# Low parts of the second mixer's a, g and k weights kept in DRAM, and its convolution taps traced at 1.2 steps per tile

## The chip, the cores and the metric

The kernel runs on one core of one Trainium2 chip. Its time is the device time of one execution in microseconds (us). The profile is of one more execution of the same program.

## What is computed

`reference` runs two blocks. The first one has two layers; each is a mixer and a feed-forward, with a post-normalisation behind each. In layer 0 the two streams (256 rows of `x` and 256 rows of context) go through everything; in layer 1 the context only gives the mixer its keys, values and states, and `x` alone goes on. The mixer projects the rows with one wide `w_in`, and merges three branches: attention, gated linear attention and a convolution of width 31 over 1024 channels. Cut to the parts of the layer 1 mixer that matter:

```python
def _latent_mixer(h, mem, cos, sin, p):
    proj = h @ p['w_in']          # k, v, kg, vg, glr | q, qg, r, glu (a and g), gates
    ...
    return _merge(o_att, o_gla, r, glu, gates, p), ...

def _conv_module(glu, p):
    a, g = jnp.split(glu, 2, axis=-1)
    y = a * jax.nn.sigmoid(g)
    y = lax.conv_general_dilated(y, p['conv_w_dw'], ...) + p['conv_b_dw']   # 31 taps, each channel alone
    y = jax.nn.silu(_layernorm(y, p['conv_ln_g'], p['conv_ln_b']))
    return y @ p['w_conv_o']
```

The second block has two smaller layers; the change doesn't touch them. All is in fp32.

## The kernel before

A product in fp32 is made of three matmuls of fp32r operands: with each operand split in a high part (a cast) and a low part (the rest), the high weights meet the high and the low rows, and the low weights meet the high rows. `mm_fm` (weights stationary, channels on the output's partitions) issues them in lines 386 to 388, `mm_tm` (rows stationary) in lines 467 to 469. Weights come as raw fp32 (`load_raw`, line 354, 1 MB for 256 columns, two buffers), and `wsplit` makes `whi` by a ScalarE cast (line 362) and `wlo` by a VectorE subtract (line 288), 128x1024 at a time and with three buffers each. `fm` does so for `mm_fm`, `proj_tm` for `mm_tm`. Every DMA is issued on SP's queue.

Nearly all else (activations, tables, intermediate rows) lies in a pool `u` of 71 slots of 2 KB per partition. A scheduler orders the instructions of all engines ahead of time in a simulated time, by priorities that follow the order in which the program traces them; `self.pri(d)` shifts the priority, and a negative d is earlier. Slow work beside the matmuls is traced by "lanes": `bg(name, generators, rate)` starts one, and each tile of a projection calls `tick`, which traces `rate` steps of every lane; `flush` traces what is left.

The mixer of layer 1 (`mixer(1, ...)`) goes as follows. Eight tiles of a and eight of g (each a product of 128 columns by 256 rows: 8 blocks x 3 matmuls), alternating two and two. After the first pair, `conv_taps` loads the convolution's weights (`cwr`, line 1307), TensorE transposes them (line 1311) and VectorE writes `cw`. After each pair of channels m, m+1 the lane "conv" gets a generator `conv`: its taps `ca<-gt,cw,ca` (line 291, at priority +600) come in 15 steps of 4, so 60 steps in all at `CRATE1` = 1.0 steps for each tile. Then k and v (4 tiles), q (8), the small gate rows (1), kg (4), qg (4), vg (8), and merge(0) (16 tiles: 8 gates and 8 of `w_att_o`), which give 12 ticks of the a/g stage after its first four tiles and 45 more. After merge(0), `flush("gla", "conv")` traces the taps that are left; the last step of the last pairs sums the channels into `cs` on GpSimd. Then `conv_norm` runs in the lane: TensorE sums the columns of `cs` (line 1347), and squares, scale and low parts follow, while merge(2) computes its gates and then needs the result for `w_conv_o`. The scores of the gated linear attention (`eq`, `ek`: GpSimd, VectorE, ScalarE) are traced in the same stretch.

The feed-forward of layer 0 (about 840 to 1160 us) has two halves of `ffn_up` (12 and 10 pairs of tiles of 128 columns by 512 rows) with a down projection between them: 24 + 12 + 20 = 56 ticks. The lane "ada" (loads `aw`, 256 KB each) runs there. `flush("ada")` stands behind it.

Of the kernel before, what the change touches and what calls it, by code (L numbers as in the profile page):

```python
# [9 lines left out]
F32 = mybir.dt.float32  # L10
# [15 lines left out]
CRATE1 = 1.0  # L26
# [4 lines left out]
CP = 600  # L31
PLO0A = 0
# [155 lines left out]
class Builder:  # L188
    NU = 71

    def __init__(self, ctx, tc, ins, out, dbg=None, stop=None):
        self.tc, self.nc, self.I, self.out = tc, tc.nc, ins, out
        self.dbg, self.stop = dbg, stop
        self.n = 0
        self.lanes = {}
        self.pool_lo = 0
        self.nsplit = 0
        self.wpri = WP
        self.behind = None
        self.fheld = None  # L200
        self.spare = {}
        self.lo_behind = []
        self.hook = self.lo_after = None
        self.ns = [None]
        P = lambda **k: ctx.enter_context(tc.tile_pool(**k))
        self.cp = P(name="cp", bufs=1)
        self.sp = P(name="sp", bufs=12)
        self.up = P(name="up", bufs=self.NU)
        self.wp = P(name="wp", bufs=2)
        self.rp = P(name="rp", bufs=2)  # L210
        self.hp = P(name="hp", bufs=3)
        self.lp = P(name="lp", bufs=3)
        self.pm = P(name="pm", bufs=3, space=PSUM)
        self.ps = P(name="ps", bufs=5, space=PSUM)
# [142 lines left out]
    def wsplit(self, src, shape, pri=None):  # L357
        hi = self.hp.tile(list(shape), F32R, tag="whi", name=self.nm("whi"))
        lo = self.lp.tile(list(shape), F32R, tag="wlo", name=self.nm("wlo"))
# [9 lines left out]
    def fm(self, w, c0, ncols, nk=8):  # L369

        raw = None
        for m in range(ncols // 128):
# [3 lines left out]
            yield self.wsplit(raw[:, :, o : o + 128], (128, nk, 128))  # L376

    def mm_fm(self, out, W, a, nk=8, first=True, last=True):
# [5 lines left out]
        for k in range(nk):  # L384
            mm = self.nc.tensor.matmul
            mm(out, lhsT=hi[:, k, :], rhs=a.hi[k], start=(first and k == 0), stop=False)  # L386
            mm(out, lhsT=hi[:, k, :], rhs=a.lo[k], start=False, stop=False)  # L387
            mm(out, lhsT=lo[:, k, :], rhs=a.hi[k], start=False, stop=(last and k == nk - 1))  # L388
# [82 lines left out]
    def proj_tm(self, specs, nk, a, tts, consumer, hold=0, mid=None, between=None, ks=None, late=None, held=None, need=None, hook=False):  # L471
# [8 lines left out]
        for part, kl in enumerate((ks[: nk - hold], ks[nk - hold :])):  # L480
# [8 lines left out]
            for h, (w, r0, c0, ncols) in enumerate(specs):  # L489
                for run in runs:  # L490
# [6 lines left out]
                    for k2 in range(0, n4, 2):  # L497
# [3 lines left out]
                        hi, lo = self.wsplit(raw[:, k2 : k2 + n2, :], (128, n2, ncols))  # L501
                        for t in tts:
                            for k in range(n2):
                                kk = run[k2 + k]
                                self.mm_tm(ps[t, h], a, t, kk, (hi[:, k, :], lo[:, k, :]), kk == ks[0], kk == ks[-1])
# [1254 lines left out]
    def layer1(self, l):  # L1760
# [33 lines left out]
        if l == 0:  # L1794
            self.bg("ada", [self.ada(1, (1, 0, 4, 3, 2, 5))], AD1)
        if T == 512:
# [10 lines left out]
            self.flush("ada")  # L1807
# [373 lines left out]
```

## Time and profile before

| | us |
|---|---|
| median of 3 executions | 2539.07 |
| lowest and highest of them | 2538.33 and 2540.02 |
| the profiled execution | 2540.03 |
| its span, first to last instruction | 2538.2 |

| engine | busy us of the span | share |
|---|---|---|
| TensorE, matmul | 2405.4 | 95% |
| TensorE, weight load | 2066.3 | 81% |
| VectorE | 1624.2 | 64% |
| ScalarE | 1180.4 | 47% |
| GpSimd | 521.2 | 21% |

Shares of the whole span are means over stages with different limits. The feed-forward of layer 0 lies at 840 to 1160 us, a and g of the second mixer at 1217 to 1282, k, v and q at 1282 to 1345, attention and vg at 1345 to 1470, merge(0) at about 1470 to 1520, and merge(2) begins there. "Granted clock" is the share of full speed at which TensorE was allowed to run. In the rows PE is TensorE, PEld its weight loads, DVE VectorE, ACT ScalarE, POOL GpSimd, SP or SPq the queue that issues DMAs.

### The profile page before, as it was taken

To read this page: it belongs to the slowest core of one execution; us is meant where nothing else is said; L and a number is where in the kernel's file an instruction comes from. 1 tells how busy PE (TensorE), PEld (TensorE's weight loads), DVE (VectorE), ACT (ScalarE), POOL (GpSimd) and SP (SyncE) were. 2 spreads that over 40 slices of the span, in tenths; PEclk is the share of its full clock that TensorE was granted. 3 is DMA by queue.
4 is the path that set the end of the run, shared out by engine and by line. 5 is a ranking of instruction groups with operands and counts; after the bars stand their busy time and mean duration, and the time that the engine had idled before them with its cause. 6 is when DMAs were issued, how large, how long until landed. Compare 5 with 4: busy or idle time off the path is not lost. (4 is left out here: it accounts for less than half of the span.)

```text
span 2538.2 us, 38571 instructions
## 1 busy us (share of the span) xinstructions
PE 2405.4 (95%) x15163; PEld 2066.3 (81%) x15163; DVE 1624.2 (64%) x2700; ACT 1180.4 (47%) x2225; POOL 521.2 (21%) x460
## 2 busy tenths in 40 slices
PE   7989999899999999999889987998999999999998
PEld 4767887688877777778879887888987899887997
DVE  5878997984365433343899597676625656556564
ACT  3223577654343322232536945654443644446443
POOL 1002003790014000003310006531072100102001
PEclk9999999999999999999999998999999999999999
DMA  8432212223433545553342252643664246543454
GB/s 256 150 136 73 84 31 90 67 84 117 133 102 131 183 150 183 166 183 100 92 129 92 68 166 84 196 137 96 211 208 149 85 150 219 198 144 106 153 192 149
DMA packets 277689, 345.39 MB, mean 136 GB/s; under 512 B 12894, under 2 KB 208888, under 8 KB 277508
## 3 DMA queue, kind: packets, MB, share of 16 engines
q1 hardware_dynamic: 277508, 342.94, 41.5%
q8 instruction: 119, 1.95, 0.3%
q14 instruction: 62, 0.51, 0.1%
HBM read 341.85 MB, written 1.05 MB: 135 GB/s over the span
## 5 line engine op out<-in xcount | busy, mean ns | idle before, releaser
L386 PE MATMUL pm<-hi,whi 128*128 128x256 f32 (+1 forms) x2824 | 917.8, 327 | 24.5 <-ACT mt L298 13.1
L388 PE MATMUL pm<-hi,wlo 128*128 128x256 f32 (+1 forms) x2824 | 909.6, 323 | 6.8 <-DVE wlo L288 6.6
L387 PE MATMUL pm<-lo,whi 128*128 128x256 f32 (+1 forms) x2824 | 910.7, 323 | 4.1 <-POOL lo L288 2.7
L362 ACT CAST whi<-raw 128x1024 fp32r<-128x1024 f32 (+1 forms) x464 | 484.5, 1049 | 829.4 <-PE pm L387 518.9
L288 DVE TENSOR_TENSOR wlo<-raw,whi 128x1024 fp32r<-128x1024 f32 (+2 forms) x437 | 550.9, 1264 | 423.5 <-ACT whi L362 400.0
L386 PEld LDWEIGHTS pm<-hi,whi 128*128 128x128 f32 x2824 | 540.2, 192 | 69.8 <-ACT mt L298 13.9
L388 PEld LDWEIGHTS pm<-hi,wlo 128*128 128x128 f32 x2824 | 541.1, 192 | 52.4 <-DVE wlo L288 8.9
L387 PEld LDWEIGHTS pm<-lo,whi 128*128 128x128 f32 x2824 | 542.0, 192 | 48.3 <-issue 4.1
L291 DVE SCALAR_TENSOR_TENSOR ca<-gt,cw,ca 128x242 f32<-128x242 f32 (+28 forms) x480 | 267.4, 608 | 0.2
L467 PE MATMUL pm<-whi,hi 128*128 128x512 f32 x536 | 212.8, 397 | 7.9 <-DVE qn L288 3.6
L468 PE MATMUL pm<-wlo,hi 128*128 128x512 f32 x536 | 210.6, 393 | 8.9 <-DVE wlo L288 7.7
L469 PE MATMUL pm<-whi,lo 128*128 128x512 f32 x536 | 210.2, 392 | 0.0
L288 POOL TENSOR_TENSOR s<-s,mhalf 128x1 f32<-128x1 f32 (+2 forms) x82 | 66.9, 816 | 481.2 <-DVE s L295 474.1
L288 POOL TENSOR_TENSOR hl<-hr,hh 128x512 fp32r<-128x512 f32 (+1 forms) x38 | 56.0, 1477 | 467.4 <-ACT hh L454 328.1
L467 PEld LDWEIGHTS pm<-whi,hi 128*128 128x128 f32 x536 | 101.3, 189 | 31.3 <-issue 5.4
L468 PEld LDWEIGHTS pm<-wlo,hi 128*128 128x128 f32 x536 | 101.3, 189 | 30.0 <-DVE wlo L288 8.1
L469 PEld LDWEIGHTS pm<-whi,lo 128*128 128x128 f32 x536 | 101.2, 189 | 22.0 <-issue 0.8
L288 POOL TENSOR_TENSOR ek<-B 128x256 f32<-128x256 f32 (+1 forms) x100 | 102.0, 1039 | 1.1 <-DVE mt L288 0.6
L288 POOL TENSOR_TENSOR eq<-B 128x256 f32<-128x256 f32 x96 | 89.8, 955 | 49.0 <-DVE ptot L291 27.7
L288 POOL TENSOR_TENSOR wlo<-raw,whi 128x1024 fp32r<-128x1024 f32 (+1 forms) x35 | 81.1, 2330 | 84.3 <-ACT whi L362 78.0
L467 PE MATMUL pm<-hh,hi 128*128 128x512 f32 (+2 forms) x258 | 92.4, 361 | 4.8 <-ACT hi L768 2.3
L468 PE MATMUL pm<-hl,hi 128*128 128x512 f32 (+2 forms) x258 | 93.0, 361 | 1.3 <-POOL hl L288 0.9
(327 smaller groups left out, 3350.2 us busy)
## 6 DMA issues: line engine op xcount, KB each, us to landing
raw<-in_w_in_dram SPq DMA_DIRECT2D x84, 1024.0 KB
aw<-in_w_ada_dram SPq DMA_DIRECT2D x192, 256.0 KB
raw<-in_w_gate_up_dram SPq DMA_DIRECT2D x40, 1024.0 KB
raw<-in_w_ff_gate_dram SPq DMA_DIRECT2D x21, 1024.0 KB
raw<-in_w_ff_up_dram SPq DMA_DIRECT2D x21, 1024.0 KB
raw<-in_w_down_dram SPq DMA_DIRECT2D x20, 1024.0 KB
raw<-in_w_ff_down_dram SPq DMA_DIRECT2D x18, 1024.0 KB
raw<-in_w_att_o_dram SPq DMA_DIRECT2D x8, 1024.0 KB
```

Of the source, the lines that this page charges most:

```text
L288: return (eng or self.nc.vector).tensor_tensor(out=out, in0=a, in1=b, op=op)
L291: return self.nc.vector.scalar_tensor_tensor(out=out, in0=a, scalar=s, in1=b, op0=op0, op1=op1)
L362: self.nc.scalar.copy(hi, src)
L386: mm(out, lhsT=hi[:, k, :], rhs=a.hi[k], start=(first and k == 0), stop=False)
L387: mm(out, lhsT=hi[:, k, :], rhs=a.lo[k], start=False, stop=False)
L388: mm(out, lhsT=lo[:, k, :], rhs=a.hi[k], start=False, stop=(last and k == nk - 1))
L467: f(p, lhsT=a.hi[kk][:, sl], rhs=hi, start=first, stop=False)
L468: f(p, lhsT=a.hi[kk][:, sl], rhs=lo, start=False, stop=False)
L469: return f(p, lhsT=a.lo[kk][:, sl], rhs=hi, start=False, stop=last)
```

## The change

`lo_ahead` is a new lane "early" in the feed-forward of layer 0. Step by step it loads 256 KB of `w_in[1]` (two blocks of 128 rows by 256 columns, or one by 512 for k and v), casts, subtracts, and stores the low part to a pool `dp` in DRAM: 32 steps for a and g with two stores each, 8 for the k and v columns with one. It runs at `ERATE` = 0.8 steps per tile and is flushed with "ada". `lo_back` reads the low parts back in the second mixer, two loads of 256 KB for a tile of a or g and one for each block of k and v, at priority `LBP` = -200, into slots of `u`. `wsplit` then makes no `wlo`. `CRATE1` becomes 1.2.

```diff
--- before.py
+++ after.py
@@ -23,12 +23,14 @@
           "g": 5664, "gate": 6688}
 WP = -100
 CRATE0 = 1.3
-CRATE1 = 1.0
+CRATE1 = 1.2
 ARATE0 = 0.6
 ARATE1 = 0.6
 GRATE0 = 0.8
 GRATE1 = 0.6
 CP = 600
+ERATE = 0.8
+LBP = -200
 PLO0A = 0
 PLO0B = 0
 PLO0 = PLO0A, PLO0B
@@ -210,6 +212,8 @@
         self.rp = P(name="rp", bufs=2)
         self.hp = P(name="hp", bufs=3)
         self.lp = P(name="lp", bufs=3)
+        self.dp = P(name="dp", bufs=1, space=bass.MemoryType.DRAM)
+        self.early = {}
         self.pm = P(name="pm", bufs=3, space=PSUM)
         self.ps = P(name="ps", bufs=5, space=PSUM)
 
@@ -354,8 +358,54 @@
             self.nc.sync.dma_start(t, src)
         return t
 
-    def wsplit(self, src, shape, pri=None):
+    def lo_ahead(self, w, fms, tms):
+
+        nc = self.nc
+
+        def part(src, n, outs):
+            raw = self.u((128, n, 512 // n), F32, "er")
+            nc.sync.dma_start(raw, src)
+            hi, lo = self.u((128, n, 512 // n), F32R, "eh"), self.u((128, n, 512 // n), F32R, "el")
+            nc.scalar.copy(hi, raw)
+            self.tt(lo, raw, hi.bitcast(F32), ALU.subtract)
+            for o, c in outs:
+                nc.sync.dma_start(o, (lo[:, :, c] if n > 1 else lo[:, 0, c]).bitcast(F32))
+
+        for c0 in fms:
+            d = [[self.dp.tile([128, 4, 128], F32, name=self.nm("dl")) for _ in range(2)] for _ in range(2)]
+            for k in range(0, 8, 2):
+                part(w[k * 128 : k * 128 + 256, c0 : c0 + 256].rearrange("(k p) c -> p k c", p=128), 2,
+                     [(d[m][k // 4][:, k % 4 : k % 4 + 2, :], slice(128 * m, 128 * m + 128)) for m in range(2)])
+                if k == 6:
+                    for m in range(2):
+                        self.early[w.tensor.name, w.offset, 0, c0 + 128 * m] = d[m]
+                yield
+        for c0 in tms:
+            for k in range(8):
+                d = self.dp.tile([128, 512], F32, name=self.nm("dl"))
+                part(w[k * 128 : k * 128 + 128, c0 : c0 + 512].unsqueeze(1), 1, [(d, slice(0, 512))])
+                self.early[w.tensor.name, w.offset, k * 128, c0] = [d]
+                yield
+
+    def lo_back(self, w, r0, c0):
+
+        ds = self.early.pop((w.tensor.name, w.offset, r0, c0), None)
+        if ds is None:
+            return None
+        out = []
+        for d in ds:
+            t = self.u(d.shape, F32R, "wl")
+            with self.pri(LBP):
+                self.nc.sync.dma_start(t.bitcast(F32), d)
+            out.append(t)
+        return out
+
+    def wsplit(self, src, shape, pri=None, los=None):
         hi = self.hp.tile(list(shape), F32R, tag="whi", name=self.nm("whi"))
+        if los:
+            with self.pri(self.wpri if pri is None else pri):
+                self.nc.scalar.copy(hi, src)
+            return hi, los
         lo = self.lp.tile(list(shape), F32R, tag="wlo", name=self.nm("wlo"))
         self.nsplit += 1
         with self.pri(self.wpri if pri is None else pri):
@@ -373,7 +423,9 @@
             if m % 2 == 0:
                 raw = self.load_raw(w, 0, nk, c0 + m * 128, min(256, ncols - m * 128))
             o = (m % 2) * 128
-            yield self.wsplit(raw[:, :, o : o + 128], (128, nk, 128))
+            if m % 2 == 0:
+                ls = [self.lo_back(w, 0, c0 + (m + j) * 128) for j in range(2)]
+            yield self.wsplit(raw[:, :, o : o + 128], (128, nk, 128), los=ls[m % 2])
 
     def mm_fm(self, out, W, a, nk=8, first=True, last=True):
         if isinstance(a, Pair):
@@ -383,9 +435,10 @@
         hi, lo = W
         for k in range(nk):
             mm = self.nc.tensor.matmul
+            lk = lo[k // 4][:, k % 4, :] if isinstance(lo, list) else lo[:, k, :]
             mm(out, lhsT=hi[:, k, :], rhs=a.hi[k], start=(first and k == 0), stop=False)
             mm(out, lhsT=hi[:, k, :], rhs=a.lo[k], start=False, stop=False)
-            mm(out, lhsT=lo[:, k, :], rhs=a.hi[k], start=False, stop=(last and k == nk - 1))
+            mm(out, lhsT=lk, rhs=a.hi[k], start=False, stop=(last and k == nk - 1))
 
     def proj_fm(self, w, c0, ncols, a, T, fm=None, done=()):
 
@@ -498,11 +551,13 @@
                         n2 = min(2, n4 - k2)
                         if need:
                             need(run[k2])
-                        hi, lo = self.wsplit(raw[:, k2 : k2 + n2, :], (128, n2, ncols))
+                        ls = [self.lo_back(w, r0 + run[k2 + k] * 128, c0) for k in range(n2)]
+                        ls = [x[0] for x in ls] if all(ls) else None
+                        hi, lo = self.wsplit(raw[:, k2 : k2 + n2, :], (128, n2, ncols), los=ls)
                         for t in tts:
                             for k in range(n2):
                                 kk = run[k2 + k]
-                                self.mm_tm(ps[t, h], a, t, kk, (hi[:, k, :], lo[:, k, :]), kk == ks[0], kk == ks[-1])
+                                self.mm_tm(ps[t, h], a, t, kk, (hi[:, k, :], lo[k] if ls else lo[:, k, :]), kk == ks[0], kk == ks[-1])
                             if run[k2 + n2 - 1] == ks[-1]:
                                 consumer(t, h, ps[t, h])
                         self.tick()
@@ -1793,6 +1848,8 @@
             return
         if l == 0:
             self.bg("ada", [self.ada(1, (1, 0, 4, 3, 2, 5))], AD1)
+            cols = [IN_OFF[n] + 256 * i for i in range(4) for n in "ag"]
+            self.bg("early", [self.lo_ahead(I["w_in"][1], cols, [IN_OFF["k"]])], ERATE)
         if T == 512:
             g = self.ffn_up(wg, 0, wu, 0, 0, 12, a, T, mid)
             gates = self.gates(l, 5, xs)
@@ -1804,7 +1861,7 @@
                 self.proj_tm([(wd, 0, hf * 512, 512)], 12, g, range(4), c)
             pre = lambda: self.bg("pre", [self.prehold([(wd, 12 * 128, 512, 512)], PW3, 8, 2)])
             g = self.ffn_up(wg, 0, wu, 0, 12, 22, a, T, None, pre if PH2 else None)
-            self.flush("ada")
+            self.flush("ada", "early")
             self.a1 = Pair(self.act_alloc(8, 256), self.act_alloc(8, 256))
             part1 = lambda s: self.mod_T(1, s, 0, [nts.pop((s, t)) for t in range(2)], self.a1.parts[s], 0, False)
             last = (0, 0)
```

## Rows read from the trace of the kernel before

**Rows 1.** The page: busy us, share of the span and instructions of each engine

```profile
PE 2405.4 (95%) x15163; PEld 2066.3 (81%) x15163; DVE 1624.2 (64%) x2700; ACT 1180.4 (47%) x2225; POOL 521.2 (21%) x460
```

**Rows 2.** Busy time by stage: us, PE, PEld, DVE, ACT, POOL, PEclk, DMA share, GB/s

```profile
840.00:1160.00 320.00, 320.00 (x1513) 248.10 (x1512) 126.44 (x153) 92.93 (x124) 22.31 (x14) 1.00 0.52 175
1185.00:1225.00 40.00, 38.44 (x202) 32.69 (x201) 30.88 (x55) 12.49 (x22) 15.73 (x17) 1.00 0.09 27
1217.00:1282.00 65.00, 57.28 (x429) 54.82 (x430) 54.85 (x96) 36.36 (x65) 20.04 (x19) 0.95 0.42 126
1282.00:1345.00 63.00, 54.32 (x278) 45.22 (x277) 55.93 (x123) 24.50 (x72) 9.09 (x9) 0.97 0.37 115
1345.00:1400.00 55.00, 55.00 (x442) 54.00 (x442) 53.14 (x113) 34.89 (x70) 1.57 (x2) 1.00 0.26 82
1400.00:1470.00 70.00, 67.06 (x395) 58.74 (x393) 39.46 (x82) 67.19 (x100) 1.54 (x2) 1.00 0.25 75
1470.00:1520.00 50.00, 44.65 (x369) 44.43 (x368) 45.57 (x85) 19.94 (x26) 3.21 (x4) 0.99 0.60 189
1520.00:1560.00 40.00, 28.05 (x185) 27.00 (x187) 31.91 (x52) 26.39 (x62) 20.22 (x25) 0.75 0.17 54
```

**Rows 3.** TensorE's waits, 1210 to 1350: us in total, times, longest

```profile
PE ps L1311 <- DMA cwr<-in_conv_w_dw_dram: 3.4, 2, 2.0
...
PE pm L467 <- DVE qn L288: 2.2, 2, 1.7
PE pm L386 <- DVE qn L288: 2.2, 1, 2.2
...
PE pm L388 <- DVE wlo L288: 1.6, 1, 1.6
```

**Rows 4.** TensorE's waits, 1400 to 1565

```profile
PE pm L386 <- ACT mt L298: 13.1, 4, 6.7
PE ps L1347 <- POOL cs L288: 5.3, 1, 5.3
```

**Rows 5.** Timeline of VectorE and GpSimd, 1515 to 1555: start, us, instruction, idle before

```profile
1515.69 1.23 DVE L291 SCALAR_TENSOR_TENSOR ca<-gt,cw,ca 128x242 f32<-128x242 f32 x3
...
1553.96 0.42 DVE L288 TENSOR_TENSOR lo<-ca,hi 128x256 fp32r<-128x256 f32 x1
...
1516.71 2.72 POOL L288 TENSOR_TENSOR cs<-cs,ca 128x256 f32<-128x256 f32 x2 [106.63 <-DVE ca L291]
1519.39 1.19 POOL L288 TENSOR_TENSOR eq<-B 128x256 f32<-128x256 f32 x2
```

**Rows 6.** Busy time in slices of 5 us

```profile
1525.00:1530.00 5.00, 0.00 (x0) 0.00 (x0) 4.24 (x6) 2.69 (x8) 3.67 (x4) 0.60 0.36 114
1530.00:1535.00 5.00, 4.85 (x20) 4.50 (x21) 1.92 (x4) 0.38 (x2) 3.15 (x6) 0.50 0.30 99
```

**Rows 7.** Groups of instructions, 1217 to 1345: busy us, mean ns, idle before

```profile
L288 DVE TENSOR_TENSOR wlo<-raw,whi 128x1024 fp32r<-128x1024 f32 x28 | 34.2, 1228 | 5.2 <-ACT whi L362 5.1
```

**Rows 8.** Timeline of SP's queue, 1232 us

```profile
1232.09 0.74 SPq L1307 DMA_DIRECT2D cwr<-in_conv_w_dw_dram  x2
```

**Rows 9.** Tile hh, feed-forward: ns min/median/max; SP timeline there

```profile
L454 ACT CAST hh<-hr x8: 602/610/615, 1112.7 to 1150.3; 128x512 fp32r<-128x512 f32 x8
L288 DVE TENSOR_TENSOR hl<-hr,hh x4: 679/684/686, 1113.7 to 1146.3; 128x512 fp32r<-128x512 f32 x4
...
916.64 5.29 SPq L624 DMA_DIRECT2D aw<-in_w_ada_dram  x8
```

**Rows 10.** Waits of SP's queue, 840 to 1160

```profile
SPq L354 <- DVE wlo L288: 211.2, 24, 13.0
```

**Rows 11.** Tile ca (the taps) by stage: DVE, ACT, POOL busy, PEclk, DMA

```profile
1217.00:1282.00 65.00, 22.29 (x48) 1.09 (x2) 0.00 (x0) 0.95 0.42 126
1400.00:1470.00 70.00, 6.82 (x17) 0.00 (x0) 1.54 (x2) 1.00 0.25 75
1470.00:1518.00 48.00, 25.21 (x60) 1.20 (x2) 1.29 (x1) 1.00 0.58 182
```

## The prediction

> **What bounds the kernel now.** I read the engine shares first, then the same engines stage by stage, then who makes TensorE wait, and last the instructions around each wait. Over the whole span TensorE is busy 95% of 2538.2 us [rows 1]. The profiled execution took 2540.03 us, 1.0 us more than the median 2539.07; the sum below is made against the profiled one and then set on the median. So a few tens of us of TensorE idle time, and the stretches at a lower clock, are all that an edit which leaves the matmuls alone can win. The stages say where they lie [rows 2]. In the first feed-forward (840 to 1160) TensorE is busy all of 320.00 us at full clock, and VectorE only 126.44, ScalarE 92.93: work put on those two there should be covered. From 1217 to 1345, where the second mixer makes a, g, k, v and q, TensorE is idle 7.7 + 8.7 = 16.4 us and VectorE is busy 111 of 128. From 1345 to 1400 nothing waits, and VectorE is at 53.14 of 55. From 1400 to 1470 VectorE is idle 30.5 us and ScalarE is full (67.19 of 70). From 1470 to 1560 TensorE is idle 5.4 + 12.0 = 17.3 us, the last 40 at clock 0.75.
>
> The waits name the causes. In the first stretch they are small and of many kinds: the transposes of the convolution's weights wait for their transfer (3.4), the third matmul for a low part from VectorE (1.6), later ones for normalised q rows (2.2 and 2.2) [rows 3]. In the last one two carry it: the column sums of the convolution wait 5.3 us for GpSimd's `cs`, and merge matmuls wait 13.1 us for ScalarE's `mt` [rows 4]. The timeline of VectorE and GpSimd shows the first: the last taps run at 1515.69, 1.23 us long, then GpSimd adds `cs` (1516.71, 2.72 us) after an idle time of 106.63 us, and GpSimd's `eq` for the gated attention stands behind it in the same queue [rows 5]. The clock then falls: 0.60 while TensorE does nothing from 1525 to 1530, 0.50 in the next 5 us, when it works again [rows 6]. (The two levels are 2.4 and 1.2 GHz.) So the second mixer's tail is bounded by the end of the taps, and not by TensorE.
>
> **Low parts removed from the second mixer.** Sixteen a/g tiles and four k tiles lose their subtract. The 28 subtracts of this stretch took 1228 ns each [rows 7], so 20 x 1.228 = 24.6 us leave VectorE: 19.6 between 1217 and 1282, 4.9 after. That isn't TensorE time; only the waits behind it are. Sure to go: 1.6 us at the third matmul. Possible: the 4.4 us behind normalised q rows, if VectorE runs earlier by then; but the faster taps refill it (below). Best case: these 6.0 plus about 3 us, the TensorE time below full speed here (57.28 x 0.05 + 54.32 x 0.03 = 4.5, of which two thirds): -9. Worst: the transposes come later (next part): +6. I take the 1.6 and a third of the 4.4: **-3**.
>
> **The 40 reads that replace them.** 40 x 256 KB = 10.5 MB are read back, on SP's queue, which carries every load. Around 1185 to 1225 the DMA engines are busy 0.09 at 27 GB/s, so 300 GB/s while busy [rows 2]; at that rate the reads take 35 us, and 0.91 x 40 = 36 us are idle there. So they nearly fit, if buffers of the shared pool are free. From 1217 to 1345 another 0.58 x 65 + 0.63 x 63 = 77 us are idle. Which transfer comes before which matters more: the reads have priority -200, which lets them pass about two pairs of tiles, the loads `cwr` among them. These are issued at 1232.09 [rows 8] and TensorE already waits 3.4 us for them. A pair of a and g tiles has 2 MB of low parts: 6.7 us at 300 GB/s for each pair that stands straight ahead of `cwr`. I take nothing, since there are 36 idle us before; 0 to +13 is kept for the range and for a rival.
>
> **What is added to the first feed-forward.** 40 loads of 256 KB, 40 ScalarE casts, 40 VectorE subtracts, 72 stores. There the same cast of 128x512 takes 610 ns and the same subtract 684 ns [rows 9]: 24.4 us on ScalarE (92.93 becomes 117 of 320) and 27.4 on VectorE (126.44 becomes 154). 24+12+20 = 56 ticks at 0.8 give 44 steps, more than 40, so the lane ends before its flush. Issue: 8 loads of 256 KB took SP 5.29 us [rows 9], so 0.66 each, 112 x 0.66 = 74 us of SP's 320. Traffic: 21 MB at 175/0.52 = 337 GB/s are 62 us of DMA time, and 0.48 x 320 = 154 are idle. Queued behind a store that waits for its subtract are SP's next raw loads, then their casts and TensorE. SP waits 211.2 us here, for a raw buffer, ahead of 24 loads [rows 10]; so it isn't the limit. One such load feeds about 320/24 = 13.3 us of matmuls, is requested one load ahead, and needs 3.1 us to land (1 MB at 337), two halves of the cast of 128x512 (1.2) and of the subtract (1.4): some 7 us of slack. A step's own chain (0.8 landing, 0.61, 0.68) is 2.1 us, below 7. Bounds: 0 and +5; I take **+1**. A gain is excluded, because TensorE has no idle time there.
>
> On this the Trainium skill speaks against the change: "DMA: Bandwidth & Descriptors", section "Bandwidth", asks for DMAs of 1 MiB or more and gives 138 GB/s at 64 KB. By an estimate at that figure the 21 MB would take 152 us of the idle 154, and the feed-forward would be at its limit. The rows disagree for this kernel: eight 256 KB loads go out with raw loads in a stage that moves 337 GB/s while busy. No row shows stores of 128 KB.
>
> **Taps at 1.2 steps for each tile.** 60 steps in four pairs. Now the fourth pair can start only at tick 45 and its last steps come after tick 57; at 1.2 it starts at tick 37.5 and ends at tick 50. The rows agree with the first: 60 of its taps, 25.21 us, all lie between 1470 and 1518, and only 6.82 us of taps between 1400 and 1470, where VectorE is half idle [rows 11]. A tile is 24 matmuls, and from 1470 to 1520 one takes 44.65/369 = 0.121 us [rows 2], so 2.9 us for a tile; seven ticks less are 20 us: the last tap ends near 1497, `cs` by 1500. The chain of column sums, squares, scaling and low parts, which in the trace runs from the end of `cs` at 1519.4 to the last low part at 1554.4 [rows 5], moves up as much, and eight gate tiles (23 us) are there to cover its first part; GpSimd's `eq` isn't held any more. Of the 17.3 us of idle time, two thirds should go: the 5.3 and half of the 13.1 behind `mt`; the rest I leave to ScalarE, which holds the exponentials. The slow clock (28.05 x 0.25 = 7.0 us) I leave too. Low bound: only the 5.3, less some loss, -4. High: 17.3 + 7.0 = -24. I take **-11.5**.
>
> What it costs: in each earlier stretch 20% more taps, 4 to 5 us on VectorE. From 1282 to 1345 the four k subtracts make up for it. From 1345 to 1400 VectorE has 1.9 us left, and 5.1 come. They carry a late priority, so they should slide into 1400 to 1470, and I put **+1.5** (0 to +3) for TensorE behind VectorE.
>
> **Sum.** -3 + 1 - 11.5 + 1.5 = -12: 2528.0 against the profiled execution, 2527 against the median.
>
> **Rivals.** (a) *Slower: the reads stand ahead of `cwr`.* SP issues in order, and with 4 MB (two pairs) before `cwr` the transposes come 13 us later; TensorE stops at them, in order, with the a/g matmuls behind. Every tap needs `cw`, and 22 us of taps lie between 1247 and 1282 now; displaced into stretches where VectorE has 9 us left, they lose the tail's gain. 13 - 3 + 1 + 1.5: 2551. It decides from some 10 us, 3 MB. For it: SP's only idle DMA time comes before 1225, and `cwr` is issued after it. Against: the same hole takes nearly all 10.5 MB. The Trainium skill bears on it: "DMA: Bandwidth & Descriptors", section "Anatomy of one DMA", says any semaphore wait happens on the issuing sequencer before dispatch. By that rule a read that waits for a buffer holds `cwr` as well.
> (b) *Same: the tail is ScalarE's and GpSimd's.* Taps end early, but `mt` and the exponentials keep their order. Only the 5.3 goes, with 1.6 and the costs 2.5: -4.4, 2535.
> (c) *Slower: stores hold raw loads in the feed-forward.* Over 7 us of hold, each of the 24 loads costs its excess; 1 us each is +24 in place of +1: 2551.
> (d) *It doesn't take effect.* The low parts are looked up by tensor, offset, row and column, the same in both places, so this is excluded.
>
> **How the numbers follow.** Forecast 0.56, (b) 0.21, (a) 0.14, (c) 0.05; the rest is a larger gain. The forecast's own bounds are -9 to +6, 0 to +5, -24 to -4, 0 to +3, which hardly meet all at one end: 2514 to 2533. With (b), up to -4.4 and a few us around it, the range is 2514 to 2543; (a) and (c) stay out. 0.2% (5.1 us) is about what a measurement of this kernel can tell from no change: faster 0.64, same 0.18, slower 0.18.
>
> **What would show it.** In the profile after: no `wlo` among the a/g tiles, reads landing from 1185 to 1225; TensorE still full from 840 to 1160 (else (c)); the wait at the transposes not above 3.4 us (else (a)); taps between 1400 and 1470 up from 6.82 us, the last near 1497; the wait for `cs` gone, that for `mt` at most halved, the clock from 1520 to 1560 above 0.75 (else (b)). I am wrong if the last tap doesn't move, or if it moves and `mt` stays.

## The result and the profile after

| | us |
|---|---|
| the kernel before, median of 4 executions | 2538.72 |
| the changed kernel, median of 4 (2644.87 to 2657.19) | 2654.68 |
| ratio, 95% interval | 1.045 (1.0431 to 1.0468) |
| the changed kernel's profiled execution, and its span | 2653.57, 2651.6 |

It is 116 us slower; the forecast was 12 us faster. To see where, I read the same events in both traces. Each row below is a group of instructions by tile, with counts, the shortest, median and longest in ns, and the first and last start in us. First the kernel before: `fg` is the gate of the first feed-forward, `ga` and `gt` are a and g of the second mixer, `kg` follows its k, v and q, and `rt` follows merge(2).

```profile
L288 DVE TENSOR_TENSOR fg<-fg,pm x22: 670/689/690, 841.9 to 1160.0; 128x512 f32<-128x512 f32 x22
...
L1492 ACT COPY ga<-pm x8: 348/366/489, 1226.0 to 1272.6; 128x256 f32<-128x256 f32 x8
L291 DVE SCALAR_TENSOR_TENSOR gt<-gt,ga x8: 414/420/953, 1231.5 to 1281.5; 128x256 f32<-128x256 f32 x8
...
L1553 ACT COPY kg<-pm x8: 361/376/415, 1350.3 to 1369.0; 128x256 f32<-128x256 f32 x8
...
L298 ACT ACTIVATE rt<-pm x8: 365/374/385, 1587.6 to 1616.1; 128x256 f32<-128x256 f32 x8
```

The same rows of the changed kernel:

```profile
L292 DVE TENSOR_TENSOR fg<-fg,pm x22: 671/686/689, 838.7 to 1240.6; 128x512 f32<-128x512 f32 x22
...
L1547 ACT COPY ga<-pm x8: 366/367/372, 1306.7 to 1384.2; 128x256 f32<-128x256 f32 x8
L295 DVE SCALAR_TENSOR_TENSOR gt<-gt,ga x8: 424/426/949, 1317.1 to 1396.8; 128x256 f32<-128x256 f32 x8
...
L1608 ACT COPY kg<-pm x8: 362/370/377, 1473.0 to 1494.3; 128x256 f32<-128x256 f32 x8
...
L302 ACT ACTIVATE rt<-pm x8: 366/381/393, 1700.9 to 1727.9; 128x256 f32<-128x256 f32 x8
```

| event | before | after | later by | lost or won in the step |
|---|---|---|---|---|
| first gate of the feed-forward | 841.9 | 838.7 | -3.2 | |
| its last gate | 1160.0 | 1240.6 | 80.6 | +83.8 |
| first a of the second mixer | 1226.0 | 1306.7 | 80.7 | +0.1 |
| last g | 1281.5 | 1396.8 | 115.3 | +34.6 |
| last kg, behind k, v and q | 1369.0 | 1494.3 | 125.3 | +10.0 |
| first row gate, behind merge(2) | 1587.6 | 1700.9 | 113.3 | -12.0 |
| end of the span | 2538.2 | 2651.6 | 113.4 | +0.1 |

So the feed-forward loses 84 us, the stages of a, g, k, v and q 45, and the tail wins 12. In the tail, from the begin of merge(2) to the first row gate, TensorE was busy 52.43 of 67 us at clock 0.85; in the changed kernel it is busy 48.22 of 55 at 0.90. Busy time, granted clock, DMA share and GB/s as in [rows 2], the kernel before first:

```profile
1520.00:1587.00 67.00, 52.43 (x535) 49.81 (x534) 52.76 (x80) 38.53 (x77) 41.63 (x50) 0.85 0.27 81
```

```profile
1645.00:1700.00 55.00, 48.22 (x520) 46.65 (x521) 46.74 (x66) 34.98 (x67) 35.80 (x40) 0.90 0.38 118
```

The experiments below give each of the three to one part of the change: the lane, the reads, and the taps.

**The feed-forward.** The same columns; the stretch ends later now, at 1240. The last row is the a and g stage, which comes further down:

```profile
840.00:1160.00 320.00, 279.33 (x1245) 213.48 (x1243) 120.31 (x153) 89.83 (x125) 10.06 (x8) 0.93 0.64 204
1160.00:1240.00 80.00, 64.33 (x247) 48.52 (x248) 31.55 (x36) 23.66 (x36) 10.71 (x6) 0.82 0.42 139
1298.00:1398.00 100.00, 68.98 (x411) 63.55 (x411) 42.94 (x93) 37.30 (x66) 16.49 (x20) 0.80 0.48 160
```

Where TensorE was busy 320.00 of 320 us [rows 2], it is busy 279.33, at clock 0.93. VectorE and ScalarE haven't become full: 120.31 and 89.83 us. DMA is at 0.64. None of them is at its limit. From 840 to 1240 TensorE is idle for 56.3 of 400 us, and busy for 343.7 us with what took 320.0 before. So some 24 us of the loss are not idle time but longer matmuls, in stretches whose clock is 0.93 and 0.82. For the idle time I looked at the waits. They stand in three engines (840 to 1240; us in total, times, longest):

```profile
PE pm L439 <- DVE fg L295: 46.3, 10, 8.4
...
ACT eh L369 <- DMA er<-in_w_in_dram: 50.0, 17, 7.4
...
SPq L372 <- DVE el L292: 146.6, 34, 12.4
```

TensorE had no wait here before; now it waits 46.3 us for VectorE's `fg`, which frees its accumulators. ScalarE waits 50.0 us for the lane's loads `er`, and SP 146.6 us at the lane's stores, for VectorE's `el`. The longest of TensorE's waits shows how they hang together. Timeline of ScalarE, SP, VectorE and TensorE (start, us, instruction, and in brackets the idle time before it and what ended it):

```profile
921.03 0.38 SPq L358 DMA_DIRECT2D raw<-in_w_ff_gate_dram  x1
921.50 0.53 SPq L367 DMA_DIRECT2D er<-in_w_in_dram  x1
928.51 0.88 SPq L372 DMA_DIRECT2D dl<-el  x2
...
927.14 0.62 ACT L369 CAST eh<-er 128x512 fp32r<-128x512 f32 x1 [5.67 <-DMA er<-in_w_in_dram]
927.66 0.62 ACT L302 ACTIVATE hi<-fg 128x512 fp32r<-128x512 f32 x1
928.20 0.58 ACT L302 ACTIVATE ft<-pm 128x512 f32<-128x512 f32 x1
...
927.79 0.69 DVE L292 TENSOR_TENSOR el<-er,eh 128x512 fp32r<-128x512 f32 x1 [5.61 <-ACT eh L369]
...
929.00 0.68 DVE L295 SCALAR_TENSOR_TENSOR fg<-ft,pm 128x512 f32<-128x512 f32 x1
...
929.74 0.79 PE L439 MATMUL pm<-hi,whi 128*128 128x512 f32 x1 [8.41 <-DVE fg L295]
```

The load `er` is issued at 921.50, right behind a raw load of 1 MB. Its cast starts at 927.14, 5.6 us later; the prediction had 0.8. ScalarE comes to the cast `eh` at 921.5 and stands there 5.67 us. Behind it in the same queue stand `hi` and `ft`, which the feed-forward's own gate needs; they start at 927.66 and 928.20. VectorE stands at `el` for the cast, and behind `el` stands `fg`. TensorE runs out of free accumulators and stops for 8.41 us. SP meanwhile holds the two stores until `el` is done (928.51), and the next loads with them. When TensorE stops, the casts of the weights stop too, so the next raw load comes later, and the next `er` behind it.

The raw load ahead explains only part of the 5.6 us. A load `er` that no raw load directly precedes also takes some 3 us to the cast that waits for it, and not 0.8:

```profile
995.83 0.50 SPq L367 DMA_DIRECT2D er<-in_w_in_dram  x1
...
998.69 0.62 ACT L369 CAST eh<-er 128x512 fp32r<-128x512 f32 x1 [3.69 <-DMA er<-in_w_in_dram]
```

**The a and g stage** took 90.1 us from the first `ga` to the last `gt`, and 55.5 before. Waits of TensorE and of SP there (1290 to 1410):

```profile
PE pm L441 <- DMA wl<-dl: 13.3, 5, 4.4
PE ps L1366 <- DMA cwr<-in_conv_w_dw_dram: 5.9, 2, 5.1
...
PE pm L521 <- DMA wl<-dl: 5.3, 1, 5.3
...
SPq L358 <- ACT ga L1547: 50.1, 4, 19.1
SPq L358 <- ACT gt L302: 37.0, 4, 10.8
```

The wait for a low part from VectorE (1.6, [rows 3]) is gone; in its place TensorE waits 13.3 + 5.3 = 18.6 us for reads of low parts (the 5.3 is at the first matmuls of k and v), and 5.9 at the transposes (3.4, [rows 3]). SP stands 87 us at raw loads, whose buffers ScalarE's casts free. (The view names `ga` and `gt`, the instruction that ScalarE starts just before its cast has ended: the cast of 1305.79 ends at 1306.83, and the raw load goes out at 1306.86.) Behind each raw load stand four reads. The timeline shows the pattern:

```profile
1273.20 14.79 SPq L399 DMA_DIRECT2D wl<-dl  x4
1306.86 0.38 SPq L358 DMA_DIRECT2D raw<-in_w_in_dram  x1
1307.29 2.18 SPq L399 DMA_DIRECT2D wl<-dl  x4
1316.79 0.38 SPq L358 DMA_DIRECT2D raw<-in_w_in_dram  x1
1317.27 0.74 SPq L1362 DMA_DIRECT2D cwr<-in_conv_w_dw_dram  x2
1318.10 2.48 SPq L399 DMA_DIRECT2D wl<-dl  x4
...
1305.79 1.04 ACT L407 CAST whi<-raw 128x1024 fp32r<-128x1024 f32 x1 [2.92 <-PE pm L440]
```

That cast in turn waited for TensorE (2.92 us): a raw load waits for a cast, the cast for a matmul, and the matmuls for reads behind the raw load before.

Most of the reads didn't go where DMA was idle: the first four are out by 1288, and the next come at 1307, when the matmuls have begun. In front of the first four SP waits for slots of the shared pool, which the post-normalisation's `x` and `z` free; from 1288 to 1307 it stands at a raw load (the 19.1 above):

```profile
SPq L399 <- DVE x L292: 6.8, 2, 6.5
SPq L399 <- DVE z L292: 6.4, 1, 6.4
```

### The profile page after: what moved, and what is told of

Read it like the earlier page. It is cut to its first block, busy times and chain, and to the rows that moved or that the text cites. A ratio compares the mean times of both kernels' runs of the same rounds, so it can differ in the third digit from the quotient of the medians.

```text
span 2651.6 us, 38932 instructions
## 1 busy us (share of the span) xinstructions
PE 2447.7 (92%) x15163; PEld 2094.9 (79%) x15163; DVE 1633.0 (62%) x2720; ACT 1202.4 (45%) x2265; POOL 515.7 (19%) x460
## 5 line engine op out<-in xcount | busy, mean ns | idle before, releaser
L439 PE MATMUL pm<-hi,whi 128*128 128x256 f32 (+1 forms) x2824 | 935.8, 333 | 65.9 <-DVE fg L295 46.3
L440 PE MATMUL pm<-lo,whi 128*128 128x256 f32 (+1 forms) x2824 | 926.3, 328 | 4.3 <-POOL lo L292 2.5
L441 PE MATMUL pm<-hi,wlo 128*128 128x256 f32 (+1 forms) x2696 | 880.6, 327 | 6.1 <-DVE wlo L292 5.9
L412 ACT CAST whi<-raw 128x1024 fp32r<-128x1024 f32 x444 | 463.5, 1048 | 778.1 <-PE pm L440 529.8
L292 DVE TENSOR_TENSOR wlo<-raw,whi 128x1024 fp32r<-128x1024 f32 (+2 forms) x417 | 526.1, 1265 | 417.2 <-ACT whi L412 411.5
L439 PEld LDWEIGHTS pm<-hi,whi 128*128 128x128 f32 x2824 | 552.2, 196 | 118.5 <-DVE fg L295 50.3
L440 PEld LDWEIGHTS pm<-lo,whi 128*128 128x128 f32 x2824 | 553.7, 196 | 49.4 <-POOL lo L292 4.7
L441 PEld LDWEIGHTS pm<-hi,wlo 128*128 128x128 f32 x2696 | 522.1, 194 | 50.2 <-DVE wlo L292 8.1
L295 DVE SCALAR_TENSOR_TENSOR ca<-gt,cw,ca 128x244 f32<-128x244 f32 (+29 forms) x480 | 263.5, 606 | 0.9 <-ACT ca L302 0.7
L520 PE MATMUL pm<-whi,hi 128*128 128x512 f32 x536 | 214.0, 399 | 13.1 <-DVE qn L292 6.6
L521 PE MATMUL pm<-wlo,hi 128*128 128x512 f32 x512 | 202.1, 395 | 8.9 <-DVE wlo L292 7.7
```

Source lines behind the costliest of these rows:

```text
L292: return (eng or self.nc.vector).tensor_tensor(out=out, in0=a, in1=b, op=op)
L295: return self.nc.vector.scalar_tensor_tensor(out=out, in0=a, scalar=s, in1=b, op0=op0, op1=op1)
L412: self.nc.scalar.copy(hi, src)
L441: mm(out, lhsT=lk, rhs=a.hi[k], start=False, stop=(last and k == nk - 1))
L520: f(p, lhsT=a.hi[kk][:, sl], rhs=hi, start=first, stop=False)
L521: f(p, lhsT=a.hi[kk][:, sl], rhs=lo, start=False, stop=False)
```

## The experiments

Differences are against runs of the kernel before on the same chip in the same set: 2539.54 for the taps alone and the first three lane kernels; 2541.99 for the two kernels with half of the slack and the two with the convolution's weights earlier; 2539.85 for the three kernels with reads from the whole change on and for the one without subtracts; 2532.24 (one run) for the two with the reads later in the queue. Where one time is given without an interval, it is a single run; single runs of the kernel before lie between 2532 and 2549, so a few us between two single runs say nothing. A stage's own length, read from the traces, is steadier, and stands beside the times where they are close.

**Taps alone (taps12).** The kernel before with one number changed.

```diff
-CRATE1 = 1.0
+CRATE1 = 1.2
```

> The kernel before with CRATE1 = 1.2 alone. If the tail's gain is the taps' (the term of -11.5 in the prediction; in the changed kernel the time from the first merge gate to the first row gate fell by 12.0 us), it gives 2538.7 - 12 = about 2527, and the feed-forward stays 320 us. If the higher rate itself costs where VectorE is full (1282 to 1400), less than that: 2530 to 2540. If the loss of the changed kernel came with the rate, it is above 2560.

Measured: 2530.25 (ratio 0.9964, 0.9952 to 0.9976), 9.3 us less. The taps moved as predicted; rows of tile `ca` (VectorE's busy time first) and the waits of TensorE, as in [rows 11] and [rows 4]:

```profile
1400.00:1470.00 70.00, 26.37 (x66) 1.08 (x2) 1.54 (x2) 0.98 0.24 75
1470.00:1520.00 50.00, 7.59 (x20) 2.65 (x8) 1.55 (x2) 0.98 0.57 176
...
PE pm L386 <- ACT mt L298: 3.9, 2, 3.3
...
1476.64 1.63 POOL L288 TENSOR_TENSOR cs<-cs,ca 128x256 f32<-128x256 f32 x2 [67.78 <-DVE ca L291]
```

17 taps between 1400 and 1470 became 66, 60 behind 1470 became 20. `cs` is added at 1476.64 and not at 1516.71 [rows 5], the wait for it is gone, and that for `mt` is 3.9 us, of 13.1 [rows 4]. From the last `kg` to the first row gate the trace has 207.1 us (1368.0 to 1575.1), 11.5 less than the 218.6 before; up to the last `kg` nothing is lost.

**The lane alone (lane).** The feed-forward lane as in the change; the second mixer doesn't use its results; taps at 1.0. The edit is against the changed kernel.

```diff
-CRATE1 = 1.2
+CRATE1 = 1.0
-        ds = self.early.pop((w.tensor.name, w.offset, r0, c0), None)
+        ds = None
```

> The lane in the feed-forward alone (loads, casts, subtracts, stores), its results not used: the second mixer makes its low parts itself, the taps are at 1.0. If the feed-forward's own longer time (first to last gate 404.2 us against 320.5) is the lane's doing, 2538.7 + 84 = about 2622, and the a/g stage is as before. If reads and lane disturb each other, less: 2560 to 2600. By the prediction's sum it would be 2540.

Measured: 2619.64 (ratio 1.0319, 1.0305 to 1.0334), 80 us more. The lane by itself costs what the feed-forward lost.

**The lane without stores (lane_nostore).** As the lane alone, without the last two lines of a step.

```diff
-            for o, c in outs:
-                nc.sync.dma_start(o, ...)
```

> As the lane alone, without its 72 stores (the low parts go nowhere). If SP, held by stores that wait for their subtract (129.2 us in 31 waits in the changed kernel), is what makes the feed-forward late: below 2550. If it is ScalarE, held by casts that wait for their load (43.6 us in 15 waits), this stays and the time is 2585 to 2620. If it is traffic, half of it is gone: about 2580.

Measured: 2588.65, 49 us more. So SP's hold by stores isn't all of it. By this run alone, casts would account for 49 us and stores for 31, and half of the traffic would also fit.

**The lane with slack (lane_pipe).** Same instructions, same traffic as the lane alone. The load is traced two steps ahead of its cast, the store one step behind its subtract.

```diff
+LA, SA = 2, 1
...
+                nc.sync.dma_start(raw, src)
+            ld.append((raw, n, outs) if x else None)
+            if len(ld) > LA:
...
+                    nc.scalar.copy(hi, raw)
+                    self.tt(lo, raw, hi.bitcast(F32), ALU.subtract)
...
+                if len(st) > SA:
...
+                            nc.sync.dma_start(o, ...)
+            yield
```

> The lane alone with the same instructions and the same traffic, but each load is traced two steps ahead of its cast and each store one step behind its subtract, so that nothing at the head of a queue has to wait long. If heads of queues make the feed-forward late: 2540 to 2555, and ScalarE's wait for the loads is gone from it. If traffic or the work itself does, it stays near the lane alone, about 2622.

Measured: 2541.22, 1.7 us more, which is less than the runs of the kernel before differ in this set (2536.42 to 2542.12). The feed-forward is whole again, with all of the traffic and work in it:

```profile
840.00:1160.00 320.00, 319.14 (x1502) 246.65 (x1501) 149.38 (x189) 113.01 (x163) 23.04 (x15) 1.00 0.73 239
```

TensorE 319.14 of 320 at clock 1.00, with VectorE at 149.38, ScalarE at 113.01 and DMA at 0.73. This rules out traffic and engine time as the cause.

**Half of the slack each.** In these two either only the load is ahead (load_ahead) or only the store is behind (store_late). The edits are against the kernel with slack.

```diff
-LA, SA = 2, 1
+LA, SA = 2, 0
```

> The lane alone, with each load traced two steps ahead of its cast, and the stores right behind their subtract as in the change. If ScalarE's casts, held at the head of its queue by loads, are the cause, and the stores wait long only since the casts do: 2540 to 2550. If both holds count by themselves (49 and 31 us, by the lane without stores): about 2570.

```diff
-LA, SA = 2, 1
+LA, SA = 0, 1
```

> The lane alone, with each store traced one step behind its subtract, and the loads right ahead of their cast as in the change. If the casts' wait for loads is the cause: 2585 to 2620. If the stores' wait on SP is: 2540 to 2560.

Measured: 2544.72 with the load ahead (2.7 us more), 2595.11 with the store behind (53 more). In the first, SP's wait at the stores is still long, ScalarE's wait for the loads is gone, and TensorE hardly notices; in the second ScalarE still stands at the casts (840 to 1240):

```profile
SPq L401 <- DVE el L293: 108.7, 34, 10.2
...
ACT eh L392 <- DMA er<-in_w_in_dram: 0.4, 1, 0.4
...
PE pm L453 <- DVE fg L296: 3.6, 2, 2.8
```

```profile
ACT eh L392 <- DMA er<-in_w_in_dram: 45.1, 21, 6.7
...
PE pm L453 <- DVE fg L296: 28.8, 8, 7.9
```

The feed-forward's own length in the traces, from its first gate to its last, says the same without the rest of the run:

| kernel | first gate to last gate | us | longer by |
|---|---|---|---|
| before | 841.9 to 1160.0 | 318.1 | |
| the lane alone | 839.3 to 1238.1 | 398.8 | 80.7 |
| without stores | 842.6 to 1206.6 | 364.0 | 45.9 |
| store behind | 840.4 to 1217.0 | 376.6 | 58.5 |
| load ahead | 840.9 to 1163.9 | 323.0 | 4.9 |
| both | 839.1 to 1158.8 | 319.7 | 1.6 |

So it is the cast that waits for its load at the head of ScalarE's queue. Without that wait, stores that stand 108.7 us in SP's queue cost 4.9 us at most. The 31 us by which the run without stores was better than the lane alone are not a price of the stores by themselves; they probably make loads later, and so the casts; no run shows that step.

**The whole change with the mended lane (pipe_all).** Reads as in the change, taps at 1.2; the lane with `LA, SA = 2, 1`.

> The whole change (lane, reads, taps at 1.2) with the lane in the mended form of lane_pipe. The lane then costs some 2 us and the taps give 9. If the reads by themselves cost what the a/g and k stages of the changed kernel lost (34.6 and 6.6 us): 2539.5 + 2 - 9 + 41 = 2573. If that loss was only fallout of the late feed-forward: about 2532 or less.

Measured: 2572.83 (ratio 1.0132, 1.0113 to 1.0151), 33 us more. With 1.7 for the lane and -9.3 for the taps, the reads, less what the missing subtracts give, cost 33.0 - 1.7 + 9.3 = 40.6 us. In the changed kernel, where the feed-forward was late, these stages lost 45; so that was no fallout of the late feed-forward.

**Reads one pair ahead (pipe_ahead).** The reads of a pair are traced ahead of the raw load of the pair before; those of k and v ahead of their own raw load. The edit is against the kernel above.

```diff
+                back = lambda m: [self.lo_back(w, 0, c0 + (m + j) * 128) for j in range(2)]
+                ls = nxt if m else back(0)
+                nxt = back(m + 2) if AHEAD and m + 2 < ncols // 128 else None
...
                 raw = self.load_raw(w, 0, nk, c0 + m * 128, min(256, ncols - m * 128))
             o = (m % 2) * 128
-            if m % 2 == 0:
-                ls = [self.lo_back(w, 0, c0 + (m + j) * 128) for j in range(2)]
```

> As pipe_all, with the reads of a pair of tiles traced one pair earlier, ahead of the raw load. If the reads are late because they stand behind raw loads that wait for their buffer: 2540 to 2555. If they are late because no slot of the shared pool is free for them before the post-normalisation ends: no better than pipe_all, 2570 or more.

Measured: 2547.29, 7.4 us more, and 25 less than the run above. This is in the range that was expected if the reads are late because they stand behind raw loads that wait for their buffer.

**Reads into buffers of their own (pipe_lp).** The three `wlo` buffers, which stand empty in this stage, take the reads, instead of slots of the shared pool. A tile's reads are also traced with that tile now, where four were traced with the first tile of a pair. The lane is the mended one and the taps are at 1.2, as in the whole change above.

```diff
-            t = self.u(d.shape, F32R, "wl")
...
+        t = self.lp.tile(list(shape), F32R, tag="wlo", name=self.nm("wlo"))
```

> As pipe_all, with the reads going into the three wlo buffers that stand empty in this stage, and not into slots of the shared pool. If slots and order made the reads late: 2528 to 2540, and TensorE's waits for them (18.6 us in the changed kernel) are below 5. If the stage is short of DMA rate (a pair of tiles now needs 2 MB in 5.8 us, 362 GB/s, against 300 to 337 while busy): 2545 or more, with the DMA busy nearly all of the stage.

Measured: 2530.58 (ratio 0.9971, 0.9959 to 0.9983), 9.3 us less than before, 42 less than with slots of the pool. The a and g stage of the two kernels, pool first; first `ga` to last `gt` takes 87.9 us (1228.4 to 1316.3) and 53.3 (1224.0 to 1277.3), and the rows hold a little more on both sides:

```profile
1226.00:1317.00 91.00, 63.09 (x388) 58.51 (x387) 36.38 (x83) 32.24 (x55) 11.13 (x13) 0.81 0.51 173
```

```profile
1222.00:1278.00 56.00, 48.03 (x369) 46.22 (x368) 35.66 (x82) 30.80 (x54) 15.71 (x13) 0.94 0.82 270
```

The same stage takes 87.9 us with DMA at 0.51 and clock 0.81, or 53.3 with DMA at 0.82 and clock 0.94. So the DMA engines can bring all of it in that time, if the reads are issued early enough. TensorE waits for reads twice in the second, 1.4 us in total.

**The same buffers, later in the queue (lp_late250, lp_late0).** Only the priority of the reads differs from the run above.

```diff
-LBP = -200
+LBP = 250
```

> pipe_lp (2530.58) with the reads at priority +250 in place of -200: same buffers of their own, but the reads come later in SP's queue; the pairs behind the first stand behind the fifth raw load and later, about as in pipe_all (2572.83) or later. If place in the queue is what made pipe_all's reads late: 2555 to 2590. If it was the lack of slots in the shared pool: within 8 us of pipe_lp, 2525 to 2540.

```diff
-LBP = -200
+LBP = 0
```

> pipe_lp with the reads at priority 0: in the queue three raw loads, then eight reads, a raw load, and from there on four reads behind each raw load, the pattern of pipe_all, but one pair sooner. By place in the queue: between the two, 2530 to 2555. By slots: as pipe_lp, 2525 to 2536.

Measured: 2541.68 and 2527.4, against 2532.24 for the kernel before in this set: 9.4 us more and 4.8 less, from single runs. The time from the last gate of the feed-forward to the last `kg` holds the stages of a, g, k, v and q and little else; here it is for these kernels and for those that follow:

| kernel | last gate to last `kg` | us |
|---|---|---|
| before | 1160.0 to 1369.0 | 209.0 |
| taps alone | 1159.1 to 1368.0 | 208.9 |
| whole change, mended lane | 1162.5 to 1413.6 | 251.1 |
| reads one pair ahead | 1162.5 to 1383.6 | 221.1 |
| buffers of their own | 1158.3 to 1368.4 | 210.1 |
| the same, priority +250 | 1162.9 to 1381.5 | 218.6 |
| the same, priority 0 | 1163.7 to 1367.8 | 204.1 |
| subtracts left out | 1160.3 to 1362.3 | 202.0 |
| taps, weights earlier | 1156.1 to 1357.9 | 201.8 |
| buffers of their own, weights earlier | 1161.4 to 1365.6 | 204.2 |

In the five lane kernels above, where the change touches nothing in this stretch, it is 210.0 to 211.9; so differences of 2 or 3 us say nothing.

Priority +250 costs 8.5 us more than -200, a fifth of what the pool costs (251.1 - 210.1 = 41.0); 2541.68 lies between the two ranges that were expected. Priority 0 costs nothing and came out in the range expected if slots are the cause (2525 to 2536). An earlier place alone, with slots of the pool, takes away 30.0 of the 42.1 by which the whole change is above the kernel before. So either an earlier place or other buffers takes most of the loss away. SP's waits at raw loads for ScalarE's casts (`ga` and `gt` in the view, 1160 to 1340) are 52.8 + 33.0 us in the whole change with the mended lane, and 3.3 + 7.0 with buffers of their own at +250. Why the raw loads wait less with other buffers, by free slots or by the order that the scheduler makes of it, these runs don't tell.

**The subtracts left out (nolo).** Taps at 1.2, and no `wlo` for a, g, k and v of the second mixer. The third matmul takes the high part once more, so this kernel leaves out the low weights of these columns.

```diff
+        if self.nolo:
+            with self.pri(self.wpri if pri is None else pri):
+                self.nc.scalar.copy(hi, src)
+            return hi, hi
```

> The kernel with the taps at 1.2 alone (2530.25), and the 20 subtracts of a, g, k and v left out with nothing in their place: the third matmul uses the high part again, so the low weights of these columns are missing from the result. It is the most that any way of moving these subtracts can give. By the prediction's term -3: 2527. If VectorE's time there is worth its best case, -9: 2521. If it is worth nothing: 2530.

Measured: 2520.75 (ratio 0.9931, 0.9916 to 0.9945), 19.1 us less than before, so 9.8 less than the taps alone, give or take some 5 by the two intervals; in the table it is 208.9 - 202.0 = 6.9. This is about the most that moving these subtracts can give. The run with buffers of their own, which moves them, gets none of it: it stands where the taps alone do. With priority 0 it gets 4.8 of the 6.9, by one trace.

**The convolution's weights earlier (taps_cwr, lp_cwr).** Their two loads are issued right behind the first a tile. Once on the taps alone, once on pipe_lp.

```diff
+            if m == 0:
+                next_a = next(ai)
+                rows = None if start else self.conv_rows(l)
...
```

> The taps at 1.2 alone (2530.25), with the two loads of the convolution's weights issued ahead of the fourth raw load and not after the fifth. TensorE's wait at the transposes (2.9 us there) should go, and a little of the clock behind it: 2525 to 2528. If the matmuls behind it then wait for something else at once: 2530.

> pipe_lp (2530.58) with those two loads earlier in the same way; reads of low parts and raw loads stand before them in the queue there, so its wait of 3.3 us should go at most in part: 2526 to 2531. If the read traffic is what keeps it from the 2520.75 that leaving the subtracts out gave, it stays within 3 us of pipe_lp.

Measured: 2520.96 (ratio 0.9923, 0.9907 to 0.994) and 2528.44 (0.9953, 0.9935 to 0.9971). The first is 21 us less than the kernel before, the largest gain of all these kernels. The stretch from 1240 to 1250, where the transposes wait in the kernel with the taps alone; that kernel first:

```profile
1240.00:1245.00 5.00, 3.55 (x22) 3.01 (x21) 0.42 (x1) 0.65 (x1) 0.00 (x0) 0.73 0.38 117
1245.00:1250.00 5.00, 3.47 (x17) 3.30 (x16) 4.57 (x11) 4.58 (x11) 0.00 (x0) 0.50 0.44 123
```

```profile
1240.00:1245.00 5.00, 5.00 (x44) 5.00 (x43) 5.00 (x8) 5.00 (x12) 2.57 (x4) 1.00 0.11 14
1245.00:1250.00 5.00, 3.85 (x32) 3.65 (x31) 5.00 (x8) 3.70 (x8) 2.02 (x3) 1.00 0.61 199
```

With the taps alone TensorE waited 2.9 us for the weights, and 1.5 right behind them for `ga`; the clock was 0.73 and 0.50 in these two slices, with 22 and 17 matmuls in 5 us. In the same stretch of time it now runs at 1.00, with 44 and 32, and both waits are gone. Against the taps alone this is 11.7 us (21.0 and 9.3 to their own kernels before), where 2 to 5 were expected; the two intervals leave some 5 us of doubt, and in the table the stages differ by 208.9 - 201.8 = 7.1. On the kernel with buffers of their own it is 4.3 (13.6 and 9.3), which the intervals don't tell from nothing; in the table it is 5.9. What keeps that one from the 2520.75 isn't settled. No run has both this edit and the subtracts left out, so whether the two gains add up isn't known.

## Why the prediction was wrong, step by step

- *What bounds the kernel now*: right. The tail was bounded by the end of the taps, the feed-forward by TensorE alone.
- *What is added to the first feed-forward* (+1, bounds 0 to +5): this step failed, by 79 us. The sum of work was right: with slack, the same 40 casts, 40 subtracts, 40 loads and 72 stores cost 1.7 us. What failed is the sentence on a step's own chain, "0.8 landing, 0.61, 0.68", which took transfer time at the rate of a busy DMA for the time from issue to landing. The trace shows 5.6 us from issue to cast for a load behind a raw load, and 2.9 for one with none directly ahead. And the 7 us of slack were those of a raw load; the chain doesn't eat these but stands at the head of ScalarE's queue, ahead of `hi` and `ft`, where the slack is what TensorE's accumulators give. The prediction named what is queued behind a waiting store on SP, but not what is queued behind the waiting cast on ScalarE and the waiting subtract on VectorE. Rival (c) had the right place and the wrong queue: the stores' wait alone costs 2.7 us (load ahead; 4.9 in its trace). Its sign, TensorE no longer full from 840 to 1160, came true by another cause.
- *The rule of the Trainium skill on small DMAs*, "DMA: Bandwidth & Descriptors", section "Bandwidth", by whose figure for 64 KB the prediction's estimate filled the feed-forward: the trace doesn't bear that estimate out. The lane with slack moved all of the traffic at a DMA share of 0.73, with TensorE full. The section's figures were measured on loads issued from GpSimd; here all go out on SP's queue. The stores of 128 KB, of which the trace before showed none, are in this run too.
- *The 40 reads* (0, with +13 as bound): failed, by about 41 us if what the missing subtracts give is set against it, and by some 50 by itself, if that is 9.8. Most reads did not land in the idle stretch (1185 to 1225 before, some 80 us later in the changed kernel): the first four went out, and then SP stood at a raw load. The prediction took the idle DMA time as available and asked only whether slots were free at the end of it. Rival (a) was half right: TensorE waits longer at the transposes (5.9 against 3.4 us), but reads that come too late for their own matmul cost more (18.6).
- *The Trainium skill's rule behind rival (a)*, the same page, section "Anatomy of one DMA", that any semaphore wait happens on the issuing sequencer before dispatch: the traces agree. SP stood 87 us at raw loads, with four reads behind each, while the DMA engines were at 0.48.
- *Low parts removed* (-3, best case -9): the term is measured by leaving the subtracts out, -9.8 by the times and -6.9 by the stage's length; it was too small, and near the best case. The work behind VectorE in this stage is worth more than its named waits. The change could not win it, since the reads cost more.
- *Taps at 1.2* (-11.5 for the tail, +1.5 for full VectorE, so -10): right. In the changed kernel the tail is 12.0 us shorter; with the taps alone it is 11.5 shorter, and the kernel 9.3 faster. The way there was partly luck: the last tap was forecast near 1497 and `cs` by 1500, and `cs` was done at 1478.3, without the tail winning more. Why the taps ended so early isn't known, and whether a lower rate would do as well was not run. Rival (b), which kept `mt` where it was, is ruled out: that wait fell from 13.1 to 3.9 us.

The sum with the measured terms is +80 for the lane, +41 for the reads less subtracts, -9 for the taps: +112, against 116 measured. The difference of 4 isn't explained; the three were measured on other runs. What the prediction named as proof of being wrong, the last tap or `mt` staying where they were, did not happen: it watched the one part that held.

## What to carry to other kernels

Work put on idle engines is free only if its inputs are there when its turn comes: here a cast that waited 5.67 us for its load held the gate's own `hi` and `ft` behind it, on an engine that was busy less than a third of the stage. Trace the load steps ahead of the cast (two steps turned +80 us into +2.7, with the store one step behind +1.7), and don't issue what is prefetched behind loads that wait: an earlier place took away 30 of 42 us, buffers of its own 41. And before moving work off an engine, measure what leaving it out gives: here that was 7 to 10 us, and one number and two loads issued earlier gave 21 without moving anything.

## What the runs showed of the hardware

- A load of 256 KB took 5.6 us from issue to the cast that waited for it when it went out right behind 1 MB, and 2.9 us with no raw load directly ahead, in a stretch where the DMA engines were busy 0.64. By rate alone it would be 0.8.
- Waits of TensorE go with a lower clock behind them. In the changed feed-forward 56.3 us of idle time came with clocks of 0.93 and 0.82 and some 24 us of longer matmuls. At the transposes 2.9 us of waits and 1.5 behind them came with 0.73 and 0.50 in 10 us, where 0.50 is the lower of the two levels, 1.2 GHz; without them the clock there was 1.00 and the stage 7.1 us shorter. How much of either is the clock, the runs don't separate.
- Stores can wait long in a queue at little cost: SP stood 108.7 us at them with the load ahead, and TensorE waited 3.6 us for `fg` there.
